# Order edges on the second head group's weight load in a hybrid attention block

## The chip, the cores and the metric

The kernel runs on one NeuronCore of one Trainium2 chip. The core has four compute engines that run side by side, each with an instruction queue of its own that is worked off in order: PE (TensorE, matrix products and transposes), DVE (VectorE), ACT (ScalarE) and POOL (GpSimd). SP (SyncE) computes nothing here; its queue issues most of the DMA transfers, which run on 16 DMA engines. The metric is the device time of one execution in microseconds (us). Where several runs are given, the median stands for them.

## The reference, cut to what matters

One layer on a sequence of 2048 rows of width 1024, float32 in and out:

```python
u = rms_norm(h, norm1_w)
proj = u @ w_in                       # 1024 x 3072, columns: dq | dk | dv | sq | sk | sv
y_diff = diff_attention(...)          # 4 heads, two softmax maps each, QK-norm, T5 bias, chunk-causal
y_sb   = stick_breaking_attention(..) # 8 heads, strictly causal, running products instead of a softmax
h = h + concat(y_diff, y_sb) @ w_out
h = h + SwiGLU(rms_norm(h))           # 1024 -> 2816 -> 1024
```

The change concerns only how `w_in` gets from HBM into the form in which the projection uses it, and when. No value that is computed changes.

## The kernel before

**Tiling.** The 2048 rows are 16 row blocks of 128. The heads are worked in eight groups: groups 0 to 3 hold one differential head each, groups 4 to 7 two stick-breaking heads each. A group's projection needs 384 columns of `w_in`. Every float32 operand is held as a pair of float16 tiles, a high and a low part, and a product is three matmuls (high by high, high by low, low by high), so one row block of one group takes 8 x 3 = 24 matmuls (L326, `proj_tile`).

**Loading a group's weight.** `load_w(g)` (L285) does this for group g. `fetch_w` (L267) issues three transfers on SP's queue (L272), 512 KB each, into the raw float32 buffer `wst`, of which there is one. For every group but the first, ACT then squares the whole raw weight in one instruction over 3072 columns, with a running sum as a by-product (L190); PE and DVE spread that number over the partitions (`across`, L183 and L184, in a PSUM buffer of the `pj` pair, which the projection uses too); and POOL and DVE write the high and low parts in two halves each (L220, L221) into one of two `w16` buffers. Group 0's weight is fetched at the very start and goes another way (maxima on DVE, L193).

**The first group's row blocks.** While group 0 is projected, the rows come fresh from HBM. For row block t, `fresh(t)` loads `x` into a `z4` buffer (L674, on SP), ACT sums the squares (L226), DVE and POOL form the reciprocal root (L155, L156), and DVE scales the row block (L229). `fresh_t` transposes it on PE (L665, eight transposes of 128 columns, in two halves), ACT casts each half to float16 (L683), DVE writes the low parts (L684), and SP stores the pair to a scratch tensor `xs` (L685), from which the later groups load it (L424). `feed(t)` (L688) writes these calls out two row blocks ahead of the projection. There are nine `z4` buffers and three `xt` buffers. After each projected row block, ACT and DVE take the result out of PSUM (L361, L364, L375), and after each fourth, `proj_batch` (L387) normalises and transposes q and k (L393 to L412).

**What sets the order.** The program is written as one stream of calls. `proj_stream` (L763) projects group after group; when row block `PF` = 8 of a group has been written out, it calls `load_w` for the next group (L772, L773). The order in which each engine's queue gets its instructions is then set by a planner, when the kernel is built: it plays the program through with estimated durations and lets an instruction go ahead of others that were written earlier if its operands and buffers are free in that estimate and its engine would else be idle. On the chip the queues keep this order whatever the real durations are. An order edge (`issue_after`) is the means to hold an instruction back in it: each instruction traced inside the block must stand behind the named instruction if both are on the same engine. It makes no engine wait at run time by itself.

**After the projections.** The attention of group g runs interleaved with the projection of group g + 1. Then come the output projection and the feed-forward part with two-level block products (L1030, L1138).

Of the kernel before, what the change touches and what calls it, by code (L numbers as in the profile page):

```python
# [21 lines left out]
S, D, P = 2048, 1024, 128  # L22
# [37 lines left out]
def block(tc, a, out):  # L60
    nc = tc.nc
    PE, ACT, DVE, POOL, SP = nc.tensor, nc.scalar, nc.vector, nc.gpsimd, nc.sync
    top = ExitStack()
    with top:
# [3 lines left out]
        x = a["x"][0]  # L68
# [31 lines left out]
        def pri(k):  # L100
            def deco(f):
                @functools.wraps(f)
                def g(*args):
                    with tc.high_priority(PRI[k]) if PRI[k] else nullcontext():
                        return f(*args)
                return g
            return deco

        def nm(s):
            uid[0] += 1  # L110
            return f"{s}{uid[0]}"

        def c1(n=1, name="c"):
            t = cp.tile([P, n], F32, name=nm(name))
            return t
# [18 lines left out]
        def times(o, a_, b_, c=None):  # L134
            DVE.tensor_scalar(o[:], a_[:], b_[:], c, op0=ALU.mult, **({} if c is None else {"op1": ALU.mult}))
# [22 lines left out]
        def norm_gain(src, w):  # L158
            if src is not None:
                SP.dma_start(w, src.partition_broadcast(P))  # L160
            m, r, p, r4 = c1(), c1(), c1(), c1()
            absmax(m[:], w)
            pow2(m[:], r[:], p[:])
            DVE.tensor_scalar(r4[:], r[:], 4.0, None, op0=ALU.mult)
            DVE.tensor_scalar(w, w, r4[:], None, op0=ALU.mult)
            return r, p, r4
# [40 lines left out]
        def weight_scale(pieces, rW, pW, pt, junk=None):  # L207
            sW = sm.tile([P, 1], F32, tag="sW", name=nm("sW"))
            cols = scale_begin(pieces, junk)
            scale_end(lambda m: across(m, pt, cols), rW, pW, junk is not None, sW)  # L210
            return sW

        def split_weight(hi, lo, st, n, sW, engines="P"):
            e = pick(**{k: {"A": 0.84 * n + 200, "D": 0.53 * n + 130, "P": 1.1 * n + 100}[k] for k in engines})
            if e == "A":
                ACT.mul(hi, st, sW[:])
            elif e == "D":
                DVE.tensor_scalar(hi, st, sW[:], None, op0=ALU.mult)
            else:
                POOL.tensor_scalar(hi, st, sW[:], 0.0, op0=ALU.mult, op1=ALU.add)  # L220
            DVE.scalar_tensor_tensor(lo, st, sW[:], hi, op0=ALU.mult, op1=ALU.subtract)  # L221
            note("D", 1.05 * n + 130)

        def norm_tile(xf, xn, wgt, junk=None):
            ss = sm.tile([P, 1], F32, tag="xss", name=nm("xss"))
            ACT.activation(xn if junk is None else junk, xf, AF.Square, accum_out=ss[:])  # L226
            rs = sm.tile([P, 1], F32, tag="xrs", name=nm("xrs"))
            rstd(rs[:], ss[:], 1.0 / D, EPS)
            DVE.scalar_tensor_tensor(xn, xf, rs[:], wgt, op0=ALU.mult, op1=ALU.mult)  # L229
# [27 lines left out]
        with ExitStack() as ph1:  # L257
# [6 lines left out]
            def z4():  # L264
                return zp.tile([P, 1028], F32, tag="z4", bufs=ZB, name=nm("z4"))

            def fetch_w(g):  # L267
                st = pp.tile([P, KT, 384], F32, tag="wst", bufs=1, name=nm("wst"))
                c0 = (0 if g < 4 else 1536) + 128 * (g % 4)
                for j in range(3):  # L270
                    src = a["w_in"][0, :, c0 + 512 * j : c0 + 512 * j + 128].rearrange("(k p) n -> p k n", p=P)
                    SP.dma_start(st[:, :, 128 * j : 128 * j + 128], src)  # L272
                return st
# [10 lines left out]
            @pri("lw")  # L284
            def load_w(g, st=None):  # L285
                first = st is not None
                if not first:
                    st = fetch_w(g)
                w16 = pp.tile([P, 2 * KT * 384], F16, tag="w16", bufs=2, name=nm("w16"))
                wv = w16[:].rearrange("p (s k n) -> p s k n", s=2, k=KT)  # L290
                rW, pW = c1(), c1()
                pt = psj.tile([P, 512], F32, tag="pj", name=nm("wsc"))
                if first:
                    sW = weight_scale([st[:, :, 128 * j : 128 * j + 128] for j in range(3)], rW[:], pW[:], pt)
                else:
                    sW = weight_scale([st[:].rearrange("p k n -> p (k n)")], rW[:], pW[:], pt, w16[:, : KT * 384].bitcast(mybir.dt.bfloat16))
                kn = 1 if first else 4
                for k in range(0, KT, kn):
                    ks = slice(k, k + kn)
                    split_weight(wv[:, 0, ks, :], wv[:, 1, ks, :], st[:, ks, :], 384 * kn, sW, "ADP" if first else "P")  # L300
                t, t2, kap = c1(), c1(), c1()
                times(t, rW, r_1)
                times(t2, t, t)
                times(kap, pW, p_1)
                G = {"w": wv}
                if g < 4:
                    G["epsk"], G["rty"] = c1(), c1()
                    DVE.tensor_scalar(G["epsk"][:], t2[:], EPS * 4 * 2.0 ** -16, 1e-37, op0=ALU.mult, op1=ALU.max)
                    DVE.tensor_scalar(G["rty"][:], t[:], 2.0 * math.sqrt(EPS), None, op0=ALU.mult)
                else:  # L310
                    G["epsy"], G["kz"], G["nkz"] = c1(), c1(), c1()
                    DVE.tensor_scalar(G["epsy"][:], t2[:], EPS * 2.0 ** 28, 1e-37, op0=ALU.mult, op1=ALU.max)
                    times(kap, kap, kap)
                    DVE.tensor_scalar(G["kz"][:], kap[:], 2.0 ** -9, 2.0 ** -110, op0=ALU.mult, op1=ALU.max)
                    DVE.tensor_scalar(G["nkz"][:], G["kz"][:], -1.0, None, op0=ALU.mult)
                G["q"], G["k"], G["v"] = [], [], []
                return G
# [344 lines left out]
            def transposed(xn, o):  # L662
                tr = ps.tile([P, 512], F32, tag="sc", bufs=4, name=nm("xtr"))
                for j in range(4):
                    PE.transpose(tr[:, P * j : P * j + P], xn[:, o + P * j : o + P * j + P], id32[:])  # L665
                return tr

            @pri("fr")
            def fresh(t):
                if t < 3:  # L670
                    xf, xn = xpre[t], z4()
                else:
                    xf, xn = z4(), z4()
                    SP.dma_start(xf[:, :D], x[t * P : (t + 1) * P, :])  # L674
                norm_tile(xf[:, :D], xn[:, :D], w1[:, :D])
                return xn, t

            def fresh_t(xn, t):
                xt = pp.tile([P, 2 * D], F16, tag="xt", bufs=3, name=nm("xt"))
                for h in range(2):  # L680
                    o = 512 * h
                    tr = transposed(xn, o)
                    ACT.copy(xt[:, o : o + 512], tr[:])  # L683
                    DVE.tensor_tensor(xt[:, D + o : D + o + 512], tr[:], xt[:, o : o + 512], ALU.subtract)  # L684
                SP.dma_start(xs[t], xt[:])  # L685
                return xt

            def feed(t):  # L688
                while nx[0] < min(NT, t + AHEAD + AHN):
                    nq.append(fresh(nx[0]))  # L690
                    nx[0] += 1
                while nx[1] < min(NT, t + AHEAD):
                    ahead.append(fresh_t(*nq.pop(0)))
                    nx[1] += 1
# [17 lines left out]
                DVE.tensor_scalar(bias[:], bias[:], ikz[:], None, op0=ALU.mult)  # L712
                DVE.memset(bias[0:64, :, 192:256], MASKED)

            ahead, nq, nx = [], [], [0, 0]
            feed(0)
            Gs = {0: load_w(0, st0)}

# [44 lines left out]
            def proj_stream():  # L763
                for g in range(NG):
                    for t, _ in enumerate(proj(g, Gs[g], fresh if g == 0 else None)):
                        if g == 0 and t == 0:
                            build_bias()
                        if g == NG - 1 and t in WT:
                            if t == WT[0]:
                                rp2.extend(norm_gain(a["norm2_w"], w2))  # L770
                            load_wo(WT.index(t))
                        if t == PF and g + 1 < NG:  # L772
                            Gs[g + 1] = load_w(g + 1)  # L773
                        yield

            stream = proj_stream()
            emitted = [0]

# [567 lines left out]
```

## Time and profile before

| | |
|---|---|
| Median of three runs | 2679.39 us (2678.89 to 2686.21) |
| Profiled execution, its own time | 2682.59 us |
| Profiled execution, span of its instructions | 2680.8 us |
| PE busy | 2492.4 us, 93% |
| DVE busy | 1932.7 us, 72% |
| ACT busy | 1347.0 us, 50% |
| POOL busy | 1489.1 us, 56% |
| Mean granted PE clock | 0.984 |

Times in the profile count from the start of the span. A row of the timeline gives the start, the duration, the engine, the line, the operation, the tiles (written from read) and, in brackets, how long the engine sat idle before it and what ended that. A row of the waits gives the engine and line that waited, what released it, the total, the number of times and the longest. A row of the windows gives the busy time of each engine in one stretch, the granted PE clock as a share of full speed, the busy share of the 16 DMA engines and what they moved. A busy PE is not PE at its peak: a matmul's duration overlaps the next one's, so the pace of a run of matmuls is read from their starts.

### The profile page before, as it was taken

How to read it: one execution, taken by the hardware profiler on the slowest of the kernel's cores; microseconds unless marked ns; L12 is line 12 of the kernel's file. 1: busy time of each engine (PE TensorE's matmuls, PEld its weight loads, DVE VectorE, ACT ScalarE, POOL GpSimd, SP SyncE). 2: the span in 40 equal slices, each digit the busy share in tenths (PEclk: the TensorE clock that was granted, in tenths of full speed). 3: DMA queues.
4: the chain of work that ended last, by engine and by line, in shares of the span. 5: the costliest groups of instructions: out<-in, count | busy, mean ns of one | idle time of the engine just before them, and what ended most of it. 6: DMA issues, size and time to landing. Idle time of an engine off the chain costs nothing. (4 is left out here: it accounts for less than half of the span.)

```text
span 2680.8 us, 50579 instructions
## 1 busy us (share of the span) xinstructions
PE 2492.4 (93%) x19628; PEld 1498.6 (56%) x19628; DVE 1932.7 (72%) x3711; ACT 1347.0 (50%) x2487; POOL 1489.1 (56%) x1098
## 2 busy tenths in 40 slices
PE   6998989888988989889989899999999999999999
PEld 4655656577776776557775344444444444444444
DVE  6898969898989989877766868777685544444434
ACT  4665656567978878665644535344352112111121
POOL 2578667667767766546764656565564232322323
PEclk9999999999999999999999899999999999999999
DMA  6777697767998979987897574665649743635532
GB/s 222 213 162 181 146 200 168 179 143 184 193 179 179 185 160 209 210 191 217 218 285 282 208 250 178 255 226 202 245 183 346 293 177 143 233 141 186 195 111 95
DMA packets 619585, 534.41 MB, mean 199 GB/s; under 512 B 480640, under 2 KB 548224, under 8 KB 609104
## 3 DMA queue, kind: packets, MB, share of 16 engines
q1 hardware_dynamic: 617520, 529.09, 69.9%
q8 instruction: 154, 2.52, 0.4%
q0 software_dynamic: 512, 1.36, 0.2%
q14 instruction: 87, 0.71, 0.1%
q10 hardware_dynamic: 1312, 0.72, 0.1%
HBM read 261.08 MB, written 147.32 MB: 152 GB/s over the span
## 5 line engine op out<-in xcount | busy, mean ns | idle before, releaser
L98 POOL TENSOR_TENSOR s<-z,s 128x1024 f16<-128x1024 f32 (+7 forms) x288 | 472.0, 1647 | 142.5 <-ACT s L89 109.8
L507 PE MATMUL sc<-kT,qT 128*128 128x512 f16 (+3 forms) x1520 | 382.0, 353 | 53.3 <-DVE z L623 19.3
L622 DVE TENSOR_TENSOR_SCAN z<-z,sc 128x512 f32<-128x512 f32 (+3 forms) x320 | 352.8, 1112 | 58.6 <-ACT sc L620 38.0
L1138 PE MATMUL pd<-wd,act 128*128 128x512 f16 x1764 | 390.9, 379 | 1.2 <-DVE cg L1071 1.2
L326 PE MATMUL pj<-w,xt 128*128 128x384 f16 x1920 | 352.2, 331 | 18.8 <-ACT xt L683 6.9
L1030 PEld LDWEIGHTS <-wg 128*128 128x128 f16 x1848 | 182.0, 99 | 230.2 <-issue 16.4
L518 PE MATMUL yp<-v,aT 128*128 128x64 f16 (+1 forms) x4896 | 269.8, 204 | 41.6 <-DMA aT<-s 40.2
L518 PEld LDWEIGHTS <-aT 128*128 128x128 f16 x4896 | 237.5, 99 | 120.4 <-DMA aT<-s 52.5
L1030 PEld LDWEIGHTS <-wu 128*128 128x128 f16 x1848 | 180.7, 98 | 218.0 <-issue 2.6
L98 POOL TENSOR_TENSOR act<-cg,act 128x512 f16<-128x512 f32 x112 | 148.5, 1337 | 262.9 <-ACT act L1097 150.8
L1138 PEld LDWEIGHTS <-act 128*128 128x128 f16 x1764 | 172.8, 98 | 209.4 <-issue 2.8
L326 PEld LDWEIGHTS <-xt 128*128 128x128 f16 x1920 | 187.3, 99 | 147.5 <-issue 21.4
L89 ACT CAST s<-z 128x128 f16<-128x128 f32 (+7 forms) x215 | 173.1, 809 | 134.1 <-DMA aT<-s 40.5
L98 POOL TENSOR_TENSOR hs<-hs,cu 128x512 f32<-128x512 f32 x99 | 130.9, 1328 | 171.3 <-DVE hs L1144 70.8
L619 ACT ACTIVATE z<-sc,c 128x512 f32<-128x512 f32 (+3 forms) x320 | 210.7, 663 | 25.6 <-PE sc L507 11.7
L1097 ACT CAST act<-cg 128x512 f16<-128x512 f32 x126 | 77.3, 616 | 238.4 <-DVE cg L1103 162.7
L507 PEld LDWEIGHTS <-qT 128*128 128x128 f16 x1520 | 128.4, 99 | 121.0 <-DVE z L623 23.0
L832 PE MATMUL po<-wo,mt 128*128 128x256 f16 x1536 | 180.7, 277 | 13.9 <-DVE xf L835 8.4
L1030 PE MATMUL pm<-X,wu 128*128 128x512 f16 x792 | 180.4, 379 | 1.3 <-DVE wu L221 1.3
L1030 PE MATMUL pm<-X,wg 128*128 128x512 f16 x792 | 181.3, 382 | 0.0
L342 PE MATMUL pj<-xt,w 128*128 128x128 f16 x2304 | 175.0, 220 | 6.7 <-DVE v L364 5.7
L1144 DVE SCALAR_TENSOR_TENSOR hs<-pd,c,hs 128x512 f32<-128x512 f32 x136 | 99.0, 747 | 109.6 <-PE pd L1138 83.1
(266 smaller groups left out, 4737.6 us busy)
## 6 DMA issues: line engine op xcount, KB each, us to landing
xt<-xs SPq DMA_DIRECT2D x112, 512.0 KB, 4.3
hs<-hd SPq DMA_DIRECT2D x68, 512.0 KB, 4.5
hd<-hs SPq DMA_DIRECT2D x56, 512.0 KB, 4.7
split<-wg SPq DMA_DIRECT2D x11, 1792.0 KB, 7.8
split<-wu SPq DMA_DIRECT2D x11, 1792.0 KB, 6.7
split<-wd SPq DMA_DIRECT2D x11, 1792.0 KB, 7.2
wg<-split SPq DMA_DIRECT2D x11, 1792.0 KB, 7.3
wd<-split SPq DMA_DIRECT2D x11, 1792.0 KB, 12.2
```

The lines of the kernel that those rows point to most:

```text
L89: ACT.copy(dst, src)
L98: (DVE if e == "D" else POOL).tensor_tensor(dst, a_, b_, op)
L326: PE.matmul(pj[:, :384], lhsT=xv[:, xi, kt, :], rhs=G["w"][:, wi, kt, :], start=n == 0, stop=n == 23)
L342: PE.matmul(o, lhsT=x_ if c == 2 else w_, rhs=w_ if c == 2 else x_, start=n == 0, stop=n == 23)
L507: last = PE.matmul(sc[:, : 128 * w].rearrange("p (t n) -> p t n", n=P), lhsT=G["q"][i // 4][:, a_, i % 4, :], rhs=G["k"][q][:, b_, 0:w, :] ...
L518: PE.matmul(yp[:, y0 : y0 + wd], lhsT=aT[:, a_, :], rhs=v[:, v_ : v_ + wd], start=start and j == 0 and q == 0, stop=stop and j == nb - 1 a ...
L619: ACT.activation(om[:, lo:hi], sc[:, :w], AF.Sigmoid, scale=G["nkz"][:])
L622: DVE.tensor_tensor_scan(ov, ov, sc[:, :w], om[:, hi : hi + 1], op0=ALU.mult, op1=ALU.bypass)
L832: PE.matmul(po[:, sl], lhsT=mt[:, kt, P * xi : P * xi + P], rhs=wos[2 * h + n][wi][:, kt, :], start=q == 0, stop=q == 23)
L1030: front[0] = PE.matmul(ps_[:].rearrange("p (t n) -> p t n", n=P), lhsT=wv[:, wo, wi, 128 * kt : 128 * kt + 128], rhs=X[xo][:, :, xi, kt, : ...
L1138: front[0] = PE.matmul(po[:], lhsT=act[:, ao, xi, 128 * j : 128 * j + 128], rhs=W["d"][:, wo, wi, :], start=start and u == 0 and q == 0, s ...
L1144: DVE.scalar_tensor_tensor(dst, po[:], kd[:], src, op0=ALU.mult, op1=ALU.add)
```

## The change

`fresh` keeps the latest `x` load on SP, and `fresh_t` keeps the latest cast on ACT, both in a list `marks`. Where group 1's weight load is called (g = 0, after row block 8), `load_w(1)` is traced inside two order edges, one to each. At that point `feed` has written out row blocks 0 to 9, so the marks are the `x` load of row block 9 and the second cast of row block 9, counted from 0. Hence the three raw weight transfers of group 1 must stand behind that load on SP's queue, and the square of the raw weight behind that cast on ACT's queue. PE's, DVE's and POOL's part of `load_w(1)` has no edge; it depends on the square. The other groups' loads are as before.

```diff
-                    SP.dma_start(xf[:, :D], x[t * P : (t + 1) * P, :])
+                    marks[0] = SP.dma_start(xf[:, :D], x[t * P : (t + 1) * P, :]).ins
...
-                    ACT.copy(xt[:, o : o + 512], tr[:])
+                    marks[1] = ACT.copy(xt[:, o : o + 512], tr[:]).ins
...
-            ahead, nq, nx = [], [], [0, 0]
+            ahead, nq, nx, marks = [], [], [0, 0], [None, None]
...
                         if t == PF and g + 1 < NG:
-                            Gs[g + 1] = load_w(g + 1)
+                            with ExitStack() as later:
+                                for ins in marks if g == 0 else ():
+                                    later.enter_context(tc.issue_after(ins))
+                                Gs[g + 1] = load_w(g + 1)
```

## The prediction

> **What bounds the kernel now.** I read the head of the page first, then the waits of PE in the first 110 us, where the edited lines run, then a table of windows over that stretch, and then the timelines of PE, ACT and SP around the one long wait that this showed.
>
> ```profile
> span 2680.8 us, 50579 instructions
> PE 2492.4 (93%) x19628; PEld 1498.6 (56%) x19628; DVE 1932.7 (72%) x3711; ACT 1347.0 (50%) x2487; POOL 1489.1 (56%) x1098
> ```
>
> PE is busy for 93% of the span, so a stretch in which PE stands still is lost unless something else was going to hold PE up later anyway. The waits of PE between 17 and 110 us (engine and line, releaser, total, times, longest):
>
> ```profile
> PE pj L326 <- ACT xt L683: 6.9, 1, 6.9
> PE wsc L183 <- ACT raw L375: 1.4, 1, 1.4
> ...
> PE xtr L665 <- DVE xt L684: 0.8, 1, 0.8
> PE pj L326 <- DVE m L184: 0.7, 1, 0.7
> ```
>
> One wait outweighs all others: the projection waits once for a cast of the row block. The windows (stretch; length, busy time of PE, PE's weight loads, DVE, ACT and POOL; clock, DMA share, GB/s):
>
> ```profile
> 37.10:43.90 6.80, 0.00 (x0) 0.00 (x0) 0.45 (x2) 4.81 (x8) 1.50 (x3) 0.80 0.77 306
> 43.90:48.30 4.40, 4.35 (x15) 1.97 (x16) 3.99 (x8) 2.84 (x6) 1.26 (x3) 0.54 0.25 96
> 48.30:60.00 11.70, 11.70 (x82) 8.13 (x81) 9.38 (x15) 8.05 (x16) 1.10 (x2) 1.00 0.81 278
> 60.00:82.60 22.60, 21.29 (x147) 14.89 (x145) 16.02 (x27) 13.76 (x32) 12.19 (x11) 1.00 0.88 278
> 82.60:105.00 22.40, 20.80 (x127) 13.47 (x128) 20.95 (x34) 11.90 (x25) 12.98 (x8) 0.92 0.50 149
> ```
>
> From 37.1 to 43.9 PE does nothing and DVE 0.45 us; then PE runs for 4.4 us at 0.54 of its clock; from 48.3 to 82.6 it is busy 33.0 of 34.3 us at full clock. So this stretch is bound by PE, apart from one hole that stops DVE too. What makes the hole is seen on ACT's queue:
>
> ```profile
> 32.34 0.28 ACT L361 ACTIVATE v<-pj 128x128 f16<-128x128 f32 x1 [6.79 <-PE pj L326]
> 39.09 2.76 ACT L190 ACTIVATE w<-wst 128x3072 bf16<-128x3072 f32 x1 [6.47 <-DMA wst<-in_w_in_dram]
> 41.76 0.19 ACT L190 ACTIVATION_READ_ACCUMULATOR w<-wst 128x1 f32 x1
> 41.85 0.36 ACT L375 ACTIVATE raw<-pj 128x256 f32<-128x256 f32 x1
> 42.12 1.04 ACT L226 ACTIVATE z<-z 128x1024 f32<-128x1024 f32 x1
> ...
> 43.31 1.07 ACT L683 CAST xt<-xtr 128x512 f16<-128x512 f32 x2
> ```
>
> ACT's next instruction after 32.6 us is the square of group 1's raw weight. It waits 6.47 us for its transfer and runs until 41.9 us, and behind it stand the sum of squares of row block 3 and the casts of row block 2. On PE:
>
> ```profile
> 36.04 1.04 PE L665 MATMUL xtr<-id,z 128*128 128x128 f32 x8
> 43.95 4.45 PE L326 MATMUL pj<-w,xt 128*128 128x384 f16 x14 [6.88 <-ACT xt L683]
> 48.24 1.04 PE L665 MATMUL xtr<-id,z 128*128 128x128 f32 x8
> ...
> 66.81 4.06 PE L326 MATMUL pj<-w,xt 128*128 128x384 f16 x24
> 70.70 1.04 PE L665 MATMUL xtr<-id,z 128*128 128x128 f32 x8
> ...
> 76.68 1.04 PE L665 MATMUL xtr<-id,z 128*128 128x128 f32 x8
> ...
> 82.65 0.49 PE L183 MATMUL wsc<-id,m 128*128 128x128 f32 x2 [1.36 <-ACT raw L375]
> ```
>
> The transposes of row block 2 are through at 37.08 us; only the cast is missing, and PE has nothing else to do. SP's queue over the same stretch:
>
> ```profile
> 21.93 2.13 SPq L685 DMA_DIRECT2D xs<-xt  x2
> 29.13 3.22 SPq L272 DMA_DIRECT2D wst<-in_w_in_dram  x3
> 32.45 4.50 SPq L674 DMA_DIRECT2D z<-in_x_dram  x3
> ...
> 58.12 1.26 SPq L674 DMA_DIRECT2D z<-in_x_dram  x2
> ```
>
> SP issues nothing from 24.1 to 29.1 us, since the single raw buffer is still being read by group 0's splits, then the three weight transfers, and only then row blocks 3, 4 and 5. What is in flight is seen in the DMA issues between 28 and 33 us (size each, median time to landing), and, below the gap, in those between 57.9 and 60 us:
>
> ```profile
> wst<-in_w_in_dram SPq DMA_DIRECT2D x3, 512.0 KB, 6.4
> z<-in_x_dram SPq DMA_DIRECT2D x1, 512.0 KB, 8.9
> ...
> z<-in_x_dram SPq DMA_DIRECT2D x2, 512.0 KB, 5.1
> ```
>
> **The change, part by part.** Nothing is added or removed: the same three transfers, the same square, the same splits. Two things move, and what depends on them may move too.
>
> *The square leaves its place on ACT's queue.* Without it ACT goes from the eviction at 32.6 us to the rows that stood behind it, and is free when the transposes of row block 2 end at 37.08 us. In the row at 43.31 us the first cast precedes the first matmul by 43.95 - 43.31 = 0.64 us, so the projection starts at about 37.08 + 0.64 = 37.7 instead of 43.95: 6.2 us earlier. The bounds are 0, if another instruction takes over the wait, and 6.88, the whole wait.
>
> *The slow clock behind the hole.* The 14 matmuls from 43.95 take until 48.24, that is 4.29 us. At full clock 24 start within 70.70 - 66.81 = 3.89 us, or 0.162 us each, so 14 need 2.27 us. If the hole shrinks to 0.6 us, I take the clock to stay up, as it does through the short waits of the windows from 48.3 to 82.6: 2.0 us more, bounds 0 and 2.0. The Trainium skill, TensorE: Matmul & The Clock Gate, section "What's actually happening", says that the clock halves after about 3.4 us of idleness and comes back after about 3.4 us of work. The trace agrees in kind, with 0.54 in the window behind the hole; by the page's figure the loss would be half of 3.4 us, an estimate of 1.7 us, and the sum 0.3 us smaller.
>
> *Row blocks 3 to 5 are loaded earlier.* With the three weight transfers gone from ahead of them, nothing on SP stands between 24.1 us and their loads but the `z4` buffers; even by 3.2 us (the issue time of the weights) earlier, row block 3 would be issued at 29.2 and land by 38.1 at the 8.9 us of its row. From landing to transposes stand these (groups of the first 200 us; count, total and mean in ns):
>
> ```profile
> L229 DVE SCALAR_TENSOR_TENSOR z<-z,xrs,z 128x1024 f32<-128x1024 f32 x16 | 22.4, 1400 | 3.6 <-POOL xrs L156 3.6
> ...
> L226 ACT ACTIVATE z<-z 128x1024 f32<-128x1024 f32 x16 | 16.9, 1059 | 10.9 <-DMA z<-in_x_dram 10.9
> ...
> L156 POOL TENSOR_TENSOR xrs<-xrs,mh 128x1 f32<-128x1 f32 x16 | 8.8, 553 | 43.1 <-DVE xrs L155 43.1
> ```
>
> With 0.2 us for the read of the sum that is 1.06 + 0.2 + 0.55 + 1.4 = 3.2 us, so row block 3 can be transposed at about 41.3, when row block 2's matmuls, 24 x 0.162 = 3.9 us from 37.7, end at 41.6. It follows just in time. I count nothing for it; if the load were late by 3 us, PE would lose up to those 3 us.
>
> *The transfers go behind row block 9's load.* That load is one of the two issued at 58.12 us. The weights then take 3.2 us of SP's time, and what is queued behind them is the load of row block 10 and the stores L685. Row block 10's transposes are those at 76.68 us; its load at 5.1 us and the 3.2 us chain need 8.3 us, so a load issued at 62.6 instead of 58.8 still has 14 us, of which 6 are to spare. The DMA engines are 0.88 busy from 60 to 82.6 us against 0.77 in the hole. Against the change speaks the Trainium skill, DMA: Bandwidth & Descriptors, section "Issuing engines are not separate DMA queues": all transfers run on the same 16 DMA engines and interleave, so the weights' bytes are not hidden from the row blocks, only put beside others. By that rule row blocks 10 to 12 would land later by the time of 1.57 MB; the trace bears it out where the weights ran beside row block 3, which took 8.9 us against 5.1. In rows, that lateness is 3.8 us per load, less than the 6 to spare. What it may cost is a block of ACT's queue by a late sum of squares. Such a wait stands in the timeline:
>
> ```profile
> 72.75 1.06 ACT L683 CAST xt<-xtr 128x512 f16<-128x512 f32 x2
> 75.76 0.38 ACT L375 ACTIVATE raw<-pj 128x256 f32<-128x256 f32 x1 [1.95 <-DVE v L364]
> 80.04 1.06 ACT L226 ACTIVATE z<-z 128x1024 f32<-128x1024 f32 x1 [3.89 <-DMA z<-in_x_dram]
> ...
> 82.19 0.41 ACT L375 ACTIVATE raw<-pj 128x256 f32<-128x256 f32 x1
> ```
>
> ACT waited 3.89 us for row block 13, and PE paid 1.4 of them (its wait for L375 above). So the price of late row blocks is between 0 and 3.9 us. I take 0.7, half of what PE paid here, since the loads before it have time to spare.
>
> *The square goes behind row block 9's cast.* That is the pair at 72.75 us, done at 73.8. ACT is idle there for 1.95 us before 75.76 and for 3.89 us before 80.04. The square and its read take 2.76 + 0.19 = 2.95 us, so the eviction at 75.76 comes 1.0 us later and the rest goes into the second idle time. PE, with row block 7 and its transposes to do until 77.7, does not see that 1.0 us. I count 0, bounds 0 and 2.95. If the idle time is gone, because row block 13's load comes earlier, it is up to 2.95.
>
> *Who needs the result.* The spread over the partitions (L183) stands on PE's queue after row block 8, at 82.65 us in the wait above, although the square was done at 41.9. Squared by about 76.8, it is still in time, by 5.9 us. The splits follow as before:
>
> ```profile
> 93.73 3.06 POOL L220 TENSOR_SCALAR w<-wst,sW 128x1536 f16<-128x1536 f32 x2
> 98.52 2.51 DVE L221 SCALAR_TENSOR_TENSOR w<-wst,sW,w 128x1536 f16<-128x1536 f32 x1
> ```
>
> They end at 101.0 us, so group 2's transfers, which wait for the raw buffer, are not delayed either. The gain at the front reaches the end if the later work only shifts; DVE stood still in the hole too, so it shifts with PE.
>
> *The sum*: -6.2 - 2.0 + 0.7 = -7.5 us. Against the profiled execution's 2682.6 us that is 2675.1; this execution is 3.2 us above the median of the runs, so against the median of 2679.4 I say 2672 us, 0.28% faster. About 0.3%, 8.0 us, is what a measurement of this kernel can tell from no change; it lies at 2671.4, practically at the forecast, so the chances of the two sides of that line are nearly even.
>
> **The rivals.**
>
> *More is gained.* The small stalls behind 82.6 us depend on the same neighbourhood: 1.4 + 0.8 + 0.7 us of waits, and a clock of 0.92 over 22.4 us, which is 1.8 us. If the order of the queues there comes out better too, 4.7 us go with the 8.2 of the hole, and the time is 2679.4 - 12.9 = 2666.5. For it speaks that a late L375 causes the first; against it that the weights' traffic now stands close by.
>
> *The wait moves with the square.* The planner put the square where its estimate had the transfer landed, and was 6.47 us off. If it is off again, ACT stops behind row block 9's cast. Issued by 62.6 and landed 6.4 us later, the weights are there at 69.0, 4.8 us ahead of 73.8. The rival needs a lateness of more than that, and of 6.5 us more to cost what it does now; then 6.9 + 2.0 us come back and the gain is gone: 2680, no change.
>
> *The attention stage comes out slower.* The planner decides on estimated times, and another front gives it another state for all that follows. The place is the stretch of the attention:
>
> ```profile
> 100.00:1150.00 1050.00, 939.49 (x10876) 678.08 (x10875) 927.18 (x2177) 751.24 (x1622) 740.70 (x543) 0.98 0.84 179
> ```
>
> PE is idle there for 110.5 us, in many short waits on casts, scans and transposes whose order is the planner's. If that grows by 7%, 7.5 us, the gain is used up, which is the point where it decides; if by 15%, 16.6 us, the time is 2672 + 16.6 = 2688.5, slower by 0.34%. Against it speaks that the edges hold only four instructions, and that all the rows behind them keep their dependences; for it, that a list of 50,000 instructions has no reason to fall in the same order twice.
>
> That the change does nothing is excluded as far as the trace goes: both the transfers at 29.13 and the square at 39.09 stand ahead of the marks.
>
> **How the numbers follow.** The hole closes and the lead is kept, 2668 to 2677 us: 0.50, of which 0.26 lies beyond the 0.3% line. More is gained: 0.20. The wait moves, no change: 0.10. The attention stage slower by over 0.3%: 0.20. So faster 0.26 + 0.20 = 0.46, within 0.3% 0.24 + 0.10 = 0.34, slower 0.20. The range goes from 2660, where the second case also shortens the attention stage's idle time by 6% (6.6 us), to 2692, where the third lengthens it by 18% (20 us). It leaves out about 2 in 10. The likeliest case's own range is 2668 to 2677.
>
> **What would show it.** In the profile after, PE's wait for a cast should be gone from 37 us and the clock be 1.00 in the windows from 37 to 48; ACT should cast row block 2 at about 37; SP should issue row block 3 before any group 1 weight, and the weights behind two to four more loads at about 50 us; the square should start without a wait for a transfer, some 66 to 70 us into the span; group 1's splits should end about 7 us earlier, near 94. The forecast is wrong if the square waits again, if row blocks 3 to 5 land late for want of `z4` buffers, or if the idle time of PE in the attention stage changes by more than some 7 us either way.

## The result: the hole closes, and the kernel is 1.1% slower

| | before | after |
|---|---|---|
| Median of four runs each | 2679.99 us (2678.89 to 2686.21) | 2711.93 us (2708.16 to 2712.78) |
| Profiled execution, its own time | 2682.59 us | 2708.16 us |
| Ratio after to before | | 1.0109, 95% interval 1.0094 to 1.0124 |

The loss is 32 us; 2672 was predicted, and the range ended at 2692. The two profiled executions lie less far apart, 24.4 us by their spans, and what follows is an account of those. The head of the page after:

```profile
span 2705.2 us, 50573 instructions
PE 2496.1 (92%) x19628; PEld 1504.4 (56%) x19628; DVE 1929.9 (71%) x3711; ACT 1349.3 (50%) x2487; POOL 1498.4 (55%) x1098
```

Every engine has as many instructions as before, and almost the same busy time. Of the 24.4 us between the two spans, 3.7 are longer work of PE and 20.7 are idle time of PE.

**The front.** PE's waits of the kernel after, from 17 to 110 us:

```profile
PE xtr L665 <- DVE z L229: 7.3, 5, 3.2
PE pj L326 <- ACT raw L375: 1.8, 2, 1.2
PE wsc L183 <- ACT raw L375: 0.8, 1, 0.8
PE pj L326 <- ACT xt L683: 0.2, 1, 0.2
```

The wait for the cast went from 6.9 us to 0.2. In its place PE's transposes wait for the scaled row block (L229), 7.3 us in five pieces, of which two, 1.0 us together, were there before. The windows of the prediction, in the kernel after:

```profile
37.10:43.90 6.80, 4.23 (x26) 3.13 (x25) 2.90 (x6) 2.94 (x7) 1.15 (x2) 0.90 0.59 203
43.90:48.30 4.40, 4.40 (x24) 2.51 (x23) 3.83 (x8) 2.98 (x6) 1.04 (x2) 0.77 0.52 208
...
60.00:82.60 22.60, 19.36 (x125) 12.35 (x124) 14.05 (x22) 14.19 (x28) 9.25 (x9) 1.00 1.02 298
82.60:105.00 22.40, 19.17 (x119) 12.58 (x118) 19.85 (x32) 10.92 (x25) 16.26 (x9) 0.92 0.45 156
```

From 37.1 to 48.3 us PE works for 8.6 us where it worked for 4.4. But from 60 to 105 us it works for 38.5 us where it worked for 42.1, and so gives 3.6 of the 4.3 us back. What stands behind this is on the timelines of PE, ACT and SP:

```profile
42.45 1.95 PE L665 MATMUL xtr<-id,z 128*128 128x128 f32 x8 [2.33 <-DVE z L229]
...
100.11 1.56 PE L665 MATMUL xtr<-id,z 128*128 128x128 f32 x8 [3.23 <-DVE z L229]
101.47 5.28 PE L326 MATMUL pj<-w,xt 128*128 128x384 f16 x24
```

```profile
68.92 1.07 ACT L683 CAST xt<-xtr 128x512 f16<-128x512 f32 x2 [3.75 <-DMA xs<-xt]
...
73.12 1.06 ACT L683 CAST xt<-xtr 128x512 f16<-128x512 f32 x2
74.07 2.78 ACT L190 ACTIVATE w<-wst 128x3072 bf16<-128x3072 f32 x1
```

```profile
56.15 4.67 SPq L272 DMA_DIRECT2D wst<-in_w_in_dram  x3
60.92 2.05 SPq L685 DMA_DIRECT2D xs<-xt  x2
```

The square starts without a wait, straight behind the cast of row block 9. But a cast at 68.92 waits 3.75 us for a store from its `xt` buffer, and the stores stand behind the weight transfers on SP's queue. And at 100.11 PE waits 3.23 us for a scaled row block and then runs 24 matmuls in 5.28 us, where 24 took 4.06 before: a second, smaller hole of the same kind. The scaling that it waits for (L229, started at 97.69) stood on DVE's queue straight behind both halves of group 1's split, which took 4.16 us.

**Behind the front.** PE's matmuls were counted in both traces, and the two spans cut where PE had done nearly the same number (they differ by up to 8). Windows before, then after (the columns are those of the prediction's windows):

```profile
147.00:679.00 532.00, 476.19 (x4580) 329.21 (x4579) 461.05 (x1294) 335.02 (x840) 382.66 (x273) 0.98 0.77 171
679.00:1101.00 422.00, 377.28 (x5624) 294.72 (x5619) 382.36 (x659) 350.97 (x631) 304.59 (x226) 0.99 0.95 188
1101.00:1451.00 350.00, 312.07 (x3042) 242.50 (x3039) 247.44 (x421) 196.65 (x336) 190.14 (x132) 0.96 0.86 237
```

```profile
150.70:686.80 536.10, 477.23 (x4581) 329.68 (x4579) 456.86 (x1296) 337.95 (x842) 385.05 (x275) 0.97 0.80 172
686.80:1131.30 444.50, 383.78 (x5614) 300.33 (x5612) 382.42 (x659) 350.37 (x630) 305.45 (x226) 0.97 0.86 178
1131.30:1474.80 343.50, 308.27 (x3044) 241.51 (x3043) 247.31 (x418) 194.69 (x332) 192.29 (x131) 0.98 0.87 240
```

After is 3.7 us behind when the first window opens, loses 4.1 in it, 22.5 in the second, and wins 6.5 back in the third; the rest of the span differs by 0.6. So the loss lies in the second window, where most of the stick-breaking groups' attention runs. Little is lost ahead of it: at PE's 5000th matmul (655 us in before) after is 1.8 us behind. In the second window PE is idle for 60.7 us against 44.7 (16.0 more), and its work takes 6.5 us longer at a clock of 0.97 against 0.99. The waits on evictions in this stretch, before (679 to 1101 us) and after (687 to 1131 us):

```profile
PE pj L342 <- DVE v L364: 5.2, 6, 2.3
...
PE wsc L183 <- DVE v L364: 3.8, 2, 3.5
...
PE sc L507 <- DVE kT L363: 0.2, 1, 0.2
```

```profile
PE sc L507 <- DVE kT L363: 14.7, 5, 4.2
PE pj L342 <- DVE v L364: 12.7, 5, 4.5
```

L363 and L364 stand in a helper that takes results out of PSUM (an eviction); for kT and v in this stretch `turned_out` calls it, for the projections of groups 4 to 6. Single waits for them are now up to 4.5 us long, where the longest was 3.5. No line of this code, and no constraint on it, was changed; only its place in the queues was.

### The profile page after: what moved, and what is told of

The parts are those of the page before. It is cut to its first block, busy times and chain, and to the rows that moved or that the text cites. A ratio compares the mean times of both kernels' runs of the same rounds, so it can differ in the third digit from the quotient of the medians.

```text
span 2705.2 us, 50573 instructions
## 1 busy us (share of the span) xinstructions
PE 2496.1 (92%) x19628; PEld 1504.4 (56%) x19628; DVE 1929.9 (71%) x3711; ACT 1349.3 (50%) x2487; POOL 1498.4 (55%) x1098
## 5 line engine op out<-in xcount | busy, mean ns | idle before, releaser
L326 PE MATMUL pj<-w,xt 128*128 128x384 f16 x1920 | 350.8, 332 | 13.5 <-ACT raw L375 8.5
L835 PE MATMUL po<-wo,mt 128*128 128x256 f16 x1536 | 180.4, 277 | 13.5 <-DVE xf L838 7.9
L543 DVE TENSOR_SCALAR_CACHE_REDUCE z<-sc,c 128x512 f32<-128x512 f32 (+3 forms) x256 | 161.4, 649 | 22.6 <-PE sc L507 22.0
```

Source lines behind the costliest of these rows:

```text
L326: PE.matmul(pj[:, :384], lhsT=xv[:, xi, kt, :], rhs=G["w"][:, wi, kt, :], start=n == 0, stop=n == 23)
L543: DVE.tensor_scalar(z[:, lo : lo + f], sc[:, :f], kz_d[:], None, op0=ALU.mult, op1=ALU.max, accum_out=mx[:, m, nx : nx + 1])
L835: PE.matmul(po[:, sl], lhsT=mt[:, kt, P * xi : P * xi + P], rhs=wos[2 * h + n][wi][:, kt, :], start=q == 0, stop=q == 23)
```

## The experiments

**How an order is held.** Several kernels below don't let the planner decide. They plan the program once, read each queue's order, and trace it a second time with an order edge from each instruction to the one before it in a wanted order. "Pinned" stands for this; in most of these kernels it shifts the line numbers by 3 or 4. Each ratio is to runs of the kernel before on the same chip, with its 95% interval; it is estimated from all runs and is not the quotient of two medians. Where a text says by how much one profile is ahead of another at a matmul of some number, the starts of PE's matmuls were counted in both traces.

**The move alone (e1).** Before's order on all queues, in which the three transfers and the square alone are taken to where the change puts them.

```diff
+def moved(plan):        # MOVED: (transfers, load of row block 9), (square, cast of row block 9)
+    out = {e: list(names) for e, names in plan.items()}
+    for names, mark in MOVED[:2]:
+        for e, order in out.items():
+            if mark in order:
+                rest = [n for n in order if n not in names]
+                p = rest.index(mark) + 1
+                out[e] = rest[:p] + names + rest[p:]
+    return out
...
+    _, _, plan = program(inputs, ())
+    nc, arrays, _ = program(inputs, (), list(moved(plan).values()))
```

> Every queue is pinned to the order of the kernel before, with order edges; only the three raw weight transfers stand behind row block 9's load and the square behind row block 9's cast, as in the changed kernel. So the change is made without a new plan. Theory A (the loss is made by the new order of everything behind the front): 2672 us, the 7.5 us of the prediction's sum, at least below 2680. Theory B (the moved transfers and the moved square cost time where they now stand): above 2680, toward 2712.

Measured: 2680.08 us, ratio 0.9999 (0.9990 to 1.0009): no loss, and no gain. So the loss doesn't come with the four instructions, as theory A has it, but neither does the gain that A named. On PE, then on ACT and SP:

```profile
40.12 0.50 PE L329 MATMUL pj<-w,xt 128*128 128x384 f16 x2 [0.24 <-ACT xt L686]
...
61.87 4.06 PE L329 MATMUL pj<-w,xt 128*128 128x384 f16 x24
...
69.92 1.91 PE L329 MATMUL pj<-w,xt 128*128 128x384 f16 x9 [3.11 <-ACT raw L378]
71.63 1.92 PE L668 MATMUL xtr<-id,z 128*128 128x128 f32 x8
73.33 3.52 PE L329 MATMUL pj<-w,xt 128*128 128x384 f16 x17
```

```profile
65.76 1.06 ACT L229 ACTIVATE z<-z 128x1024 f32<-128x1024 f32 x1 [5.29 <-DMA z<-in_x_dram]
```

```profile
54.07 3.86 SPq L275 DMA_DIRECT2D wst<-in_w_in_dram  x3
57.97 1.63 SPq L677 DMA_DIRECT2D z<-in_x_dram  x1
```

The hole is closed (0.24 us). But row block 10's load is issued at 57.97, behind the weights, and is there 7.8 us later; its sum of squares stands on ACT's queue ahead of the evictions, ACT stands still for 5.29 us, and PE waits 3.11 for L378. Then PE runs slowly: eight transposes take 1.92 us instead of 1.04, and the two runs of matmuls, by the 4.06 us of 24 (0.17 us each), some 0.4 and 0.6 us too long, 1.9 us together. So 5.0 us go again: the move closes one hole and opens another. Counted by matmuls, e1's profile is 4.9 us ahead of before's at the 200th (62 us), level at the 300th (77 us), and 2.7 ahead at the 500th (112 us), since before has small waits of its own behind 82 us. The clock in the profile is 0.87 from 66 to 73 us and 0.81 from 73 to 77, where before has 1.00 in both. The Trainium skill, TensorE: Matmul & The Clock Gate, section "What's actually happening", has the clock halved after about 3.4 us of idleness. The trace agrees in kind, but here less was enough: the clock fell behind this wait of 3.11 us, and in the kernel after behind the one of 2.33 us, where it stood at 0.50 from 43 to 45 us.

**The front of the one, the rest of the other (e2, e3).** Both plans are made, and each queue takes the one's order up to the end of group 1's weight load and the other's behind it.

```diff
+def joined(front, rest):        # MOVED[2]: the last instruction of load_w(1); names count up as written
+    out = {}
+    for e, names in front.items():
+        early = [p for p, n in enumerate(names) if int(n[2:]) <= int(MOVED[2][2:])]
+        first = names[: early[-1] + 1] if early else []
+        done = set(first)
+        out[e] = first + [n for n in rest[e] if n not in done]
+    return out
...
+    _, _, old = program(inputs, ())
+    _, _, new = program(inputs, (0, 1))
+    nc, arrays, _ = program(inputs, (), list(joined(new, old).values()))        # e2; e3: joined(old, new)
```

> Every queue has the changed kernel's order up to the last instruction of group 1's weight load and of what was written before it, and from there on the order of the kernel before. Theory A: about the kernel before, 2676 to 2684 us, since the changed kernel's profile is only some 2 us ahead at its front. Theory B: about the changed kernel, 2712 us.

> The reverse: the front of the kernel before, with its hole, and behind it the changed kernel's order. Theory A: about 2712 us (2705 to 2717), slow without the change. Theory B: about 2680 us.

Measured: e2 2688.33 us, 1.0028 (1.0016 to 1.0039); e3 2706.24 us, 1.0099 (1.0082 to 1.0116). Nearly the whole loss comes with the order of the rest, although the front of e3, with the square in its old place, is that of before. e2 lies between its two expectations, and by its profile its 0.28% is a price of the join: it is 0.2 us behind before's at PE's 300th matmul (77 us), 7.7 behind at the 400th (97 us), where the two orders meet, and 9.6 at the end, while after is 2.5 ahead at the 400th. PE's waits in e3 from 550 to 1200 us are those of after:

```profile
PE sc L510 <- DVE kT L366: 14.1, 5, 4.2
PE pj L345 <- DVE v L367: 12.7, 5, 4.5
```

Its front shows something else. The same instructions in the same order as before (e3, PE's timeline):

```profile
29.22 4.54 PE L329 MATMUL pj<-w,xt 128*128 128x384 f16 x15
...
38.77 1.04 PE L668 MATMUL xtr<-id,z 128*128 128x128 f32 x8
43.79 3.98 PE L329 MATMUL pj<-w,xt 128*128 128x384 f16 x14 [3.98 <-ACT xt L686]
```

The hole is 4.0 us, not 6.9. It ends about where it did before, at 43.8, since the square's transfer sets the end; it begins later, since 15 early matmuls took 4.54 us instead of 2.61.

**A new plan without the change (e4, e14).** Before's kernel with the 0.27 us fill of the bias (L713) written four times, or eight times, which only costs DVE 0.8 or 1.9 us. No edge; but the planner starts from another estimate.

```diff
                 DVE.memset(bias[0:64, :, 192:256], MASKED)
+                DVE.memset(bias[0:64, :, 192:256], MASKED)     # e4: three such lines more; e14: seven
```

> The kernel before with the 0.27 us fill of the bias tile written four times in place of once: 0.8 us more of DVE, nothing moved by an edge, but the planner gives another order to all queues. Theory A: off the kernel before by more than 0.3% (8 us) either way is possible, since any new order can be that far off; a time within 3 us of 2680 would speak against it. Theory B: 2680 us, within 2 us.

> Before's kernel with the bias fill of 0.27 us written eight times; no edge, another new plan. Theory (before's order is a favourable one among those that the planner comes to from slightly different starts): slower by 0.3 to 1.4%, 2687 to 2717. Rival (the fill written four times happened on a bad plan, and new plans scatter about before's on both sides): as likely under 2679 as over, or within 0.3% of it, 2671 to 2687.

Measured: e4 2708.17 us, 1.0105 (1.0087 to 1.0123); e14 2691.24 us, 1.0035 (1.0020 to 1.0050). Three superfluous fills cost 28 us, as much as the change within the intervals, and seven cost 9. The fills' own time can't explain it. What a new plan gives is not in proportion to what was edited. e4's waits from 550 to 1130 us:

```profile
PE pj L342 <- DVE v L364: 11.5, 6, 4.2
PE pj L342 <- DVE kT L364: 5.3, 2, 4.4
PE sc L507 <- DVE kT L363: 4.9, 2, 4.2
```

**The control (e5).** Before pinned to its own order. In the two traces the sequence on PE, ACT and POOL is the same throughout, and on DVE but for four one-element fills that change places with a neighbour.

```diff
+    nc, arrays, _ = program(inputs, (), list(plan.values()))
```

> Control: the kernel before with every queue pinned by order edges to the order it has anyway, so the queues hold the same instructions in the same order. All theories: 2680 us, within 0.1%. Its profile is a second look at the unchanged front: the hole before row block 2's cast should be about 4 us, as behind the unchanged front of e3, rather than the 6.9 us of the first profile, if the slower first matmuls are the usual case.

Measured: 2678.41 us, 1.0003 (0.9990 to 1.0015). Pinning costs nothing. The profiled execution has a span of 2671.8 us, 9.0 less than the profile of before, with the same instructions; its hole is 7.34 us, not the 4 that were expected:

```profile
26.47 2.61 PE L326 MATMUL pj<-w,xt 128*128 128x384 f16 x15
...
44.07 4.74 PE L326 MATMUL pj<-w,xt 128*128 128x384 f16 x14 [7.34 <-ACT xt L683]
```

**Smaller moves in before's order (e6, e7).** e6 moves the square alone; e7 moves the square and puts the transfers behind row block 5's load, not row block 9's.

```diff
-    for names, mark in MOVED[:2]:
+    for names, mark in MOVED[1:2]:                                    # e6
+    for names, mark in ((MOVED[0][0], LOADS[5]), MOVED[1]):           # e7
```

> Pinned to the order of the kernel before; only the square is moved behind row block 9's cast, the three transfers stay where they were, ahead of row block 3's load. Theory C (the hole is worth 4 to 6 us, and what took it back in e1 is row block 10's load behind the transfers): 2680 - 5 = 2675 us. Theory D (a lead of the front is lost in the attention stage whatever makes it): 2680 us, within 2 us.

> Pinned likewise; the square behind row block 9's cast, the three transfers behind row block 5's load, so that neither row blocks 3 to 5 nor row block 10 stand behind them. Theory C: 2674 us, and no long wait of ACT for row block 10. Theory D: 2680 us, within 2 us.

Measured: e6 2678.58 us, 0.9994 (0.9981 to 1.0007); e7 2677.81 us, 1.0000 (0.9989 to 1.0012). PE's wait for the cast, in e6 and then in e7, and the largest wait that e7 has from 17 to 110 us:

```profile
PE pj L329 <- ACT xt L687: 1.6, 1, 1.6
```

```profile
PE xtr L668 <- DVE z L232: 5.5, 4, 2.4
...
PE pj L329 <- ACT xt L687: 0.2, 1, 0.2
```

e7 closes the hole and e6 all but 1.6 us of it, without e1's long block of ACT, and still nothing can be measured in the whole. A gain of over 0.2% is excluded by e6's interval, and of over about 0.1% by e1's and e7's. The times are those of theory D, but that the lead is lost later isn't shown. In e7 the waits for the scaled row block (L232 here) have taken most of the hole's place: it is level with before at the 500th matmul (112 us). The profile of e6 is 3.5 us ahead there and 4.1 at the end; but that of e5, which moves nothing, is level there and 9.0 ahead at the end, so one profile of each can't tell what becomes of so small a lead.

**One edge at a time, planned anew (e8, e13).**

```diff
-                                for ins in marks if g == 0 else ():
+                                for ins in marks[:1] if g == 0 else ():     # e8: SP alone (transfers)
+                                for ins in marks[1:] if g == 0 else ():     # e13: ACT alone (square)
```

> The planner's own order, with the edge on SP's transfers alone and none on the square. The front should come out as in the changed kernel, since the square can't go ahead of its operand. If the loss is that of the order of the attention stage, the time may lie anywhere between 2670 and 2715 us, and it says how far two plans with nearly the same front differ; if the loss is made by the moved transfers, it is 2712 us.

> One edge alone, the one to row block 9's cast on ACT (the square), planned anew; the transfers have no edge. Theory (the loss is that of a new plan, whatever edit starts it): slower by 0.3 to 1.4%, 2687 to 2717, like the order edge on SP alone (2715.8) and the bias fill without any edge (2708.2), with 10 to 27 us of waits of PE for evictions of the turned projections in the stick-breaking groups. Rival (the loss belongs to the transfers' edge, and the square's edge is harmless, as it was in the pinned order at 2678.6): within 0.3%, 2672 to 2688, with 4 to 8 us of such waits.

Measured: e8 2715.8 us, 1.0137 (1.0118 to 1.0156); e13 2711.17 us, 1.0108 (1.0091 to 1.0125). Neither edge is the harmless one. e13 loses as much as the change, and the square's move that costs nothing in e6 comes with a loss of 29 us when the rest is planned anew. The loss belongs to the plan, not to the four instructions. e13's front shows one thing more. The square is gone from it (it starts at 71.69), and still there is a hole of 5.8 us; PE's wait, then ACT's queue:

```profile
PE pj L326 <- ACT xt L683: 5.8, 1, 5.8
```

```profile
40.38 1.06 ACT L226 ACTIVATE z<-z 128x1024 f32<-128x1024 f32 x1 [8.37 <-DMA z<-in_x_dram]
...
41.59 1.06 ACT L683 CAST xt<-xtr 128x512 f16<-128x512 f32 x2
```

Without an edge the transfers still go out at 29.27, ahead of row block 3's load. Where the square stood, the sum of squares of row block 3 now waits for that load, 8.37 us, with the casts of row block 2 behind it. The 1.6 us of e6 have the same cause. So the hole closes only if the transfers go too.

**The cut at another place (e9, e10).** As e3 and e2, but cut behind the load of group 4's weight, so that the late part holds the stick-breaking groups.

```diff
-        early = [p for p, n in enumerate(names) if int(n[2:]) <= int(MOVED[2][2:])]
+        early = [p for p, n in enumerate(names) if int(n[2:]) <= int(CUT[3][2:])]       # the last of load_w(4)
...
+    nc, arrays, _ = program(inputs, (), list(joined(old, new).values()))        # e9; e10: joined(new, old)
```

> Pinned: the order of the kernel before up to the load of group 4's weight (front and differential groups, some 550 us), the changed kernel's order from there on. If the loss is made in the stick-breaking groups, where the changed kernel's profile falls behind most: 2695 to 2705 us. If it is made in the differential groups: 2680 to 2687 us.

> The reverse: the changed kernel's order up to the load of group 4's weight, with the change in it, and the order of the kernel before from there on. If the loss is made in the stick-breaking groups: 2684 to 2692 us. If in the differential groups: 2705 to 2712 us.

Measured: e9 2703.22 us, 1.0076 (1.0057 to 1.0095); e10 2696.68 us, 1.0045 (1.0030 to 1.0061). The late part carries about two thirds of the loss. The other third, 0.45%, appears with the early part in e10, but not as a price of that part alone: up to PE's 3400th matmul (509 us) e10's profile is about as far behind before's as after's is, 4.8 and 5.7 us; between 513 and 534 us PE's order changes from the one to the other; and at the 3700th (550 us) e10 is 9.1 behind, where after is 0.8, and 12.4 at the end. So most of e10's loss seems to be made at the join, as in e2. e9 has the long waits on evictions, with the same two rows as e3 above; e10 has those of before:

```profile
PE pj L345 <- DVE v L367: 5.7, 7, 2.3
```

**The evictions first (e11, e12).** A test of the suspected cause: `turned_out` gets a priority of its own in the planner, in after (e11) and in before (e12).

```diff
-PRI = {..., "wm": 0}
+PRI = {..., "wm": 0, "to": 400}
...
-            @pri("po")
+            @pri("to")
             def turned_out(pq, pv, qT, kT, v, j):
```

> The changed kernel, planned anew with the evictions of the turned projections (groups 4 to 6) put first by priority. In the slow orders PE waits 22 to 27 us for these evictions on DVE, in the order of before 6 us. If these waits are the cause, they shrink below 10 us and the time falls by about 16 to 20 us, to 2692 to 2698 us. If they only go with another cause, the waits shrink and the time stays at 2705 to 2715 us.

> The same priority in the kernel before. There the waits for these evictions are only 6 us, so at most 6 us are to be had: 2674 to 2680 us if the evictions are what makes the difference between orders. If any new order of the stick-breaking groups is slow whatever its evictions do, 2695 to 2715 us.

Measured: e11 2703.1 us, 1.0075 (1.0055 to 1.0095); e12 2692.06 us, 1.0031 (1.0019 to 1.0043). In e11 the wait for kT fell from 14.7 to 4.1 us, that for v did not fall, and about 9 us came back, less than was expected if the waits were the cause and more than if they were not:

```profile
PE pj L342 <- DVE v L364: 13.8, 6, 4.5
...
PE sc L507 <- DVE kT L363: 4.1, 1, 4.1
```

In e12 the waits even grew, from 15.6 to 21.5 us (the table below), and its time lies in neither of the two ranges named. As both kernels are planned anew, they are two more plans as well as a test.

**All together.** PE's waits on the evictions of the projections (all rows on qT, kT, v and st of L363 and L364, 550 to 1200 us, added up by kernel) beside the ratio:

| order of the late part | kernels | waits, us | ratio |
|---|---|---|---|
| that of before | before, e1, e5, e6, e7 | 15.2 to 16.2 | 0.9994 to 1.0003 |
| that of before, early part new | e2, e10 | 15.7, 15.7 | 1.0028, 1.0045 |
| a new plan | e12, e14 | 21.5, 22.4 | 1.0031, 1.0035 |
| a new plan | e11 | 26.5 | 1.0075 |
| that of after | after, e3, e9 | 29.9, 30.3, 29.9 | 1.0109, 1.0099, 1.0076 |
| a new plan | e4, e8, e13 | 30.5, 31.7, 28.9 | 1.0105, 1.0137, 1.0108 |

The two go together. The 14.3 us by which after exceeds before are less than the 20 us of the late part (0.76%), so even at full price the evictions don't cover it, and e11 got 9 us back for 3.4 us less of such waits, so they are in part a sign of a worse plan, not its whole price. To move the evictions alone within an otherwise held order was not tried. What else makes the late part stays open, and so does what the early part costs without a join. It also stays open why before's plan is better than each of the seven newly planned kernels (after, e4, e8, e11 to e14), which are all slower, by 0.31 to 1.37%; seven do not tell how rare such a plan is. If before's settings had once been chosen by time, any new draw would start against a favourable one; nothing here tests that.

## Why the prediction was wrong

**The hole's mechanism: half right, its size a single draw.** The square held up the cast, and with both moves the wait is 0.2 us. But the prediction gave the 6.2 us to the square alone, with 0 as the bound if another instruction takes over the wait, and counted nothing for the transfers. e13 is that bound: the square gone and the transfers not, the sum of squares of row block 3, which in the rows shown stood ahead of the casts, took over a wait of 5.8 us. And for the 6.2 us, other executions with the square in its old place had 3.1 (e4), 4.0 (e3) and 7.3 (e5), as the start depends on early matmuls, 15 of which take 2.61 us in one execution and 4.54 in another. The projection started at 39.62, not at 37.7, for this reason.

**The slow clock: half right.** In e1, 12 matmuls behind the closed hole take 2.12 us, full pace. In after, a wait of 2.33 us for row block 3 followed instead, the clock fell behind it, and the window from 43.9 to 48.3 stood at 0.77, not 1.00.

**Row blocks 3 to 5 "just in time": the bound came true.** Nothing was counted, with up to 3 us as the bound; after paid 2.33 us in one place, e1 0.31.

**The price of late row blocks: mis-sized.** 0.7 us was taken; e1 shows 3.1 us of waiting and 1.9 of slow work, 5.0. The wait lies within the bounds given, 0 to 3.9 us, but the slow work behind it was not priced. The lateness was no more than estimated, 3.8 us per load: the three loads next behind the weights took 8.0 us in the median, against 5.1. What failed is the step that gave row block 10 six us to spare: it measured the slack up to the transposes on PE. The first reader on the critical side is the sum of squares on ACT, and behind it in ACT's queue stand the evictions, which PE needs at once. In after the stores did a like thing: the `xt` buffer came free 3.75 us late, and PE waited 1.2 us for the eviction behind that cast, a cost for which the prediction named the queue (the stores L685 behind the weights) but no price.

**The square's new place and the splits: right, but 4 us later.** It started at 74.07 straight behind the cast, without a wait for its transfer, though behind the latest time named, 70, since the cast that it follows came at 73.12. The weights went out at 56.15, not at about 50. Group 1's splits end at 97.8 (before 101.0, forecast about 94):

```profile
93.61 4.16 DVE L221 SCALAR_TENSOR_TENSOR w<-wst,sW,w 128x1536 f16<-128x1536 f32 x2
```

**"The gain at the front reaches the end if the later work only shifts": this step failed.** The later work did not shift. It was planned anew, and the rival that named this ("the attention stage comes out slower") is what happened, at the place given for it, with idle time growing by 16.0 us in the second window alone (13.5 over the prediction's own stretch, 100 to 1150 us) where 7.5 was given as the point of turning. It put 16.6 us on top of 2672, where 40 were measured; with seven of seven new plans slower by over 0.3%, its chance of 0.20 was too low. "The edges hold only four instructions" was counted against it; e4 shows that no held instruction is needed at all. Even with the rest held, the gain did not reach the end: e1, e6 and e7 stand at 0.9994 to 1.0000 for a forecast of 0.9972.

## What to carry to other kernels

Where a planner orders the queues, any edit is two changes: the one that is meant, and a new draw of the whole order; only a kernel with the old order held and one thing moved prices the first, and a control with a meaningless edit prices the second. If a good order has been found, keep it as an order, since here every plan made from a slightly different start was slower. When a transfer is delayed, measure its slack to the place of its first reader in that reader's queue, with all that stands behind it there, and not to the engine that needs the data in the end.

## What the runs showed of the hardware

The early matmuls run at two paces, although the windows show a clock of 1.00 for both. The windows from 28 to 34 us of before, then of e1:

```profile
28.00:34.00 6.00, 6.00 (x33) 3.04 (x32) 3.68 (x21) 0.28 (x1) 3.31 (x6) 1.00 0.71 195
```

```profile
28.00:34.00 6.00, 6.00 (x18) 2.33 (x17) 2.56 (x16) 0.00 (x0) 2.05 (x4) 1.00 0.60 183
```

33 matmuls and 18 fill the same 6 us; the same run of 15 takes 2.61 us in e5 and 4.54 in e3. The 1.00 says little here: the windows count a stretch without a clock record as full, and the first record of a trace, which grants the full clock, starts at 27.5 us in before, 22.0 in e5, 32.3 in after, 33.2 in e3 and 33.6 in e1. Behind it matmuls of 384 columns start every 0.16 us, ahead of it (seen in all of these but e5) every 0.32. So a start at half pace is common to them, and what differs is when it ends. What decides that was not controlled, and the hole behind takes up the difference, since its end is fixed by a transfer.

Nor does the length of a wait alone decide whether the clock falls. In after it fell to 0.50 behind a wait of 2.33 us; in e7 it stood at 1.00 behind waits of 2.16 and 2.39 us (windows from 45 to 47 and from 50 to 52 us).

And two executions with one and the same order (the profiles of before and of e5) differ by 9.0 us in span, which is more than the effect that was predicted.
